# A hybrid attention block on one core: the compression in rounded floats, its second layer inside the attention loop, other places for value chunks and rotary tables, and low parts moved from GpSimd to VectorE

## The chip, the cores and the metric

The kernel runs on one core of one Trainium2 chip. The metric is the device time of one execution in microseconds (us), as the median of several runs. Names of engines: PE is TensorE, DVE is VectorE, ACT is ScalarE, POOL is GpSimd, SP is SyncE (here only a DMA queue).

## The reference

Two layers (DEPTH = 2) over 512 tokens of width 1024. Each has a mixer of two attentions and a convolutional feed-forward part:

```python
def compress_blocks(k, pe, w1, b1, w2):
    blocks = k[:, idx] + pe[None, None, :, None, :]      # 31 blocks of 32 tokens, stride 16
    flat = jnp.transpose(blocks, (0, 1, 3, 2, 4)).reshape(B, n_cmp, Hkv, CMP_BLOCK * hd)
    return jax.nn.gelu(flat @ w1 + b1, approximate=True) @ w2

def nsa_attention(...):          # 8 query heads, 2 key heads: compressed, selected and window branch
    kc = compress_blocks(k_cmp, ck_pe, ck_w1, ck_b1, ck_w2)
    vc = compress_blocks(v_cmp, cv_pe, cv_w1, cv_b1, cv_w2)
    ...
    o = g[..., 0:1] * o_cmp + g[..., 1:2] * o_slc + g[..., 2:3] * o_win

def stick_breaking_attention(q, k, v):
    ...
    log_1m = jnp.where(strict, -jax.nn.softplus(z), 0.0)
    later = lax.cumsum(log_1m, axis=3, reverse=True) - log_1m
    w = jnp.where(strict, jnp.exp(jax.nn.log_sigmoid(z) + later), 0.0)

def hybrid_mixer(h, positions, ...):
    q_nsa, kv_nsa, g_nsa, qkv_sb, g_merge = jnp.split(h @ w_in, cuts, axis=-1)
    ...                          # rotary embedding of q and of two of three keys and k_cmp
    y = g_a * (o_nsa @ w_proj_nsa) + g_b * (o_sb @ w_proj_sb)
    return y @ w_out
```

All of it is in float32.

## The kernel before

**Products.** Most matrix products run in rounded floats (`fp32r`). Each operand is split in a high part, rounded, and a low part, the rest, and a product is three matmuls: high x high, low x high, high x low. The first and second layer of the compression are an exception: they run in plain floats (line 703 and the ones behind it), for which the trace has two records per matmul.

**Weights.** `Weights` goes through one list of weight tiles in the order of use. A tile of 128 x 1024 floats comes by DMA on SP's queue into one of three buffers (`wraw`). ACT rounds it (`whi`, line 95), and DVE or POOL makes the low part (`wlo`, line 96) as the tile's item says; two buffers each for whi and wlo, or a place that the item names (`dest`: "held" slots such as `sa`, `vs0`, in which a tile stays for longer). `ensure` splits tiles ahead of their use, at high priority. The order in which each engine's instructions stand is written by a scheduler which simulates a time line and follows these priorities; an engine then runs its queue in that order.

**Stages of a layer.** (1) The head: six tiles of 128 output columns (two keys, two queries, the keys and the values to be compressed), first for 256 tokens (`head_first`), then for the others (`head_second`). In layer 0 the rotary tables are computed beside it by the generator `rope_tables`, whose steps are spread over the head's matmuls; they are written to DRAM (`rot`) and read back into `cs_t`, from which layer 1 reads them too. (2) Each of the six banks is emptied: `rope` copies it (rf, line 599), turns halves around by DMA (rs), multiplies by `cs_t` (lines 603 and 606); the last bank, with the values to be compressed, is emptied by `kd` (line 660) alone. (3) The values `vN`, from three chunks of weights; the four accumulators take the banks that come free first. (4) Two more query tiles, and the compression: 16 matmuls each for keys and values (line 703) from `cstk` and the weights `cw`, gelu into `hid`, and the second layer into `kc` and `vc`. (5) The NSA loop: 32 pieces of attention, for which POOL scales P and DVE and ACT do the rest, with projections of the next stage as fill; the scores of the compressed branch are made in its steps 0 to 3 (`cmp_scores`), their transposes in step 4. (6) Stick-breaking attention (`run_heads`): Z = scores, softplus into `sbt` (line 1027) with the diagonal masked by POOL (line 995), split in `sph` (line 1032) and `spl` (line 1033), sums on PE, exp into `sbw`, masked by POOL, split in `wh` (line 1050) and `wl` (line 1051), product with the values. Its fill is `sb_pair` (sbz, line 745; qlo and sbst, line 753) and the gates (line 766). (7) Projections and output product, (8) the feed-forward part.

Of a layer's 36 tiles of `w_m` POOL makes the low parts of 28, numbers 8 to 35; DVE makes the others. Slots have one tag each and pass from tile to tile: `vn` holds vN up to the stick-breaking stage.

## Time and profile before

| what | before |
|---|---|
| median of 3 runs | 1673.69 us (1669.89 to 1676.96) |
| profiled execution | 1679.35 us |
| span in it, first to last instruction | 1677.7 us |
| mean granted clock of PE, share of full | 0.988 |
| PE busy | 1621.3 us (97%) |
| DVE busy | 1117.1 us (67%) |
| ACT busy | 814.4 us (49%) |
| POOL busy | 280.6 us (17%) |

PE is busy nearly all the time. A busy PE is not always a fast one: a matmul counts as busy at either clock, so the granted clock has to be read beside it.

### The profile page before, as it was taken

Reading aid. Unit: us, or ns where it says so; the run is one execution under the profiler, and the core shown is the slowest. Engines: PE = TensorE matmul, PEld = TensorE weight load, DVE = VectorE, ACT = ScalarE, POOL = GpSimd, SP = SyncE. Lnnn points to the kernel's source line nnn. Section 1 sums busy time; section 2 is a strip of 40 time slices with the busy share of each in tenths; the row PEclk is TensorE's granted clock in tenths of the full one; section 3 lists DMA queues with packets and bytes.
Section 4 is the critical chain, followed back from the end, with each engine's and each line's share of the span. In section 5 each row is a group of like instructions: output and inputs, shape, how many; then the busy total and the mean of one; then the engine's idle time right before and its main releaser. Section 6 shows DMA issues by size and latency. Waiting matters only on the chain. (4 is left out here: it accounts for less than half of the span.)

```text
span 1677.7 us, 23285 instructions
## 1 busy us (share of the span) xinstructions
PE 1621.3 (97%) x9034; PEld 1402.1 (84%) x9034; DVE 1117.1 (67%) x1613; ACT 814.4 (49%) x1326; POOL 280.6 (17%) x277
## 2 busy tenths in 40 slices
PE   8999999999999999999998999999999999999997
PEld 8888887778998888888897788878789988888897
DVE  7776666767588777723757667577575697776235
ACT  4555565545554444423544555574546454444233
POOL 0135454330000000000001354454200000000000
PEclk9999999999999999999998999999999999999999
DMA  5621112113422332233655111121144133333344
GB/s 190 175 86 63 40 39 63 51 62 127 130 72 76 101 101 90 96 93 116 195 162 145 63 51 52 38 63 51 51 152 138 38 101 93 97 100 95 94 126 141
DMA packets 53358, 159.96 MB, mean 95 GB/s; under 512 B 6528, under 2 KB 12160, under 8 KB 52992
## 3 DMA queue, kind: packets, MB, share of 16 engines
q1 hardware_dynamic: 50512, 149.91, 28.8%
q10 hardware_dynamic: 1584, 4.38, 0.8%
q0 software_dynamic: 1152, 4.19, 0.7%
q8 instruction: 71, 1.16, 0.3%
q14 instruction: 39, 0.32, 0.1%
HBM read 144.82 MB, written 4.72 MB: 89 GB/s over the span
## 5 line engine op out<-in xcount | busy, mean ns | idle before, releaser
L95 ACT CAST whi<-wraw 128x1024 fp32r<-128x1024 f32 (+3 forms) x241 | 246.3, 1022 | 338.0 <-PE bk L368 256.7
L96 DVE TENSOR_TENSOR wlo<-wraw,whi 128x1024 fp32r<-128x1024 f32 (+2 forms) x185 | 217.7, 1177 | 178.7 <-ACT whi L95 176.7
L368 PE MATMUL bk<-h_hi,wlo 128*128 128x512 f32 (+1 forms) x768 | 288.4, 376 | 5.8 <-DVE wlo L96 5.8
L368 PE MATMUL bk<-h_hi,whi 128*128 128x512 f32 (+1 forms) x768 | 289.0, 377 | 4.5 <-ACT rf L599 2.4
L368 PE MATMUL bk<-h_lo,whi 128*128 128x512 f32 (+1 forms) x768 | 288.7, 376 | 2.6 <-DVE h_lo L457 2.6
L368 PE MATMUL f<-h_hi,whi 128*128 128x512 f32 x448 | 183.1, 409 | 9.3 <-DVE sbz L745 6.7
L368 PE MATMUL f<-h_lo,whi 128*128 128x512 f32 x448 | 178.5, 398 | 0.0
L368 PE MATMUL f<-h_hi,wlo 128*128 128x512 f32 x448 | 178.2, 398 | 0.0
L96 POOL TENSOR_TENSOR wlo<-wraw,whi 128x1024 fp32r<-128x1024 f32 x56 | 139.2, 2485 | 211.8 <-ACT whi L95 194.2
L368 PEld LDWEIGHTS bk<-h_hi,wlo 128*128 128x128 f32 x768 | 146.8, 191 | 32.3 <-DVE wlo L96 7.1
L368 PEld LDWEIGHTS bk<-h_hi,whi 128*128 128x128 f32 x768 | 147.2, 192 | 30.2 <-ACT rf L599 2.6
L368 PEld LDWEIGHTS bk<-h_lo,whi 128*128 128x128 f32 x768 | 146.8, 191 | 28.2 <-DVE h_lo L457 3.2
L368 PE MATMUL bk<-ah,wlo 128*128 128x256 f32 (+1 forms) x484 | 161.8, 334 | 2.5 <-DVE wlo L96 2.5
L368 PE MATMUL bk<-ah,whi 128*128 128x256 f32 (+1 forms) x484 | 160.4, 331 | 0.0
L368 PE MATMUL bk<-al,whi 128*128 128x256 f32 (+1 forms) x484 | 160.2, 331 | 0.0
L368 PEld LDWEIGHTS f<-h_hi,whi 128*128 128x128 f32 x448 | 85.4, 191 | 29.4 <-DVE sbz L745 8.1
L368 PEld LDWEIGHTS bk<-ah,wlo 128*128 128x128 f32 x484 | 91.8, 190 | 12.6 <-DVE wlo L96 3.4
L1189 DVE TENSOR_TENSOR cu<-bk,r 128x512 f32<-128x512 f32 x88 | 60.2, 687 | 61.1 <-PE bk L368 60.9
L368 PEld LDWEIGHTS f<-h_hi,wlo 128*128 128x128 f32 x448 | 85.5, 191 | 17.8
L368 PEld LDWEIGHTS bk<-ah,whi 128*128 128x128 f32 x484 | 91.9, 190 | 8.7
L368 PEld LDWEIGHTS bk<-al,whi 128*128 128x128 f32 x484 | 91.9, 190 | 8.6
L368 PEld LDWEIGHTS f<-h_lo,whi 128*128 128x128 f32 x448 | 85.5, 191 | 15.1
(233 smaller groups left out, 3252.0 us busy)
## 6 DMA issues: line engine op xcount, KB each, us to landing
wraw<-in_w_u SPq DMA_DIRECT2D x88, 512.0 KB, 3.5
wraw<-in_w_m SPq DMA_DIRECT2D x72, 512.0 KB, 3.4
wraw<-in_w_d SPq DMA_DIRECT2D x44, 512.0 KB, 3.6
wraw<-in_w_d SPq DMA_DIRECT2D x22, 384.0 KB, 3.1
wraw<-in_w_pr SPq DMA_DIRECT2D x16, 512.0 KB, 3.6
wraw<-in_w_o SPq DMA_DIRECT2D x16, 512.0 KB, 3.6
rs<-rf SPq DMA_DIRECT2D x56, 64.0 KB, 3.0
cw<-in_cw ACTq DMA_DIRECT2D x2, 1024.0 KB, 6.1
```

The costliest lines, as they stand in the source:

```text
L95: self.nc.scalar.copy(hi[:, c], raw[:, c])
L96: eng.tensor_sub(lo[:, c], raw[:, c], hi.bitcast(F)[:, c])
L368: return nc.tensor.matmul(o, a, b, start=first, stop=last, skip_group_check=True)
L1189: nc.vector.tensor_mul(u, b, r2)
```

## The change

Five things. The compression's weights become two ordinary items of the weight list, 1024 columns each, split and laid out so that the high and low part of 64 output rows stand side by side (`fold`); the moving operand is split too, so one matmul of 128 x 132 makes all four partial products, and the halves are added afterwards. The second layer (`cb`, `kc`, `vc`) moves into `finish_compression`, called in step 2 of the NSA loop, and `cmp_scores` begins in step 2, with two of its parts per step. The three value chunks get places of their own (`q1`, `on`, `sa`) and are asked for during the second half of the head. The rotary tables stay in SBUF (`rtab`, in the slot `vn`) in layer 0, and layer 1 loads them by POOL's queue; the table's computation starts eight steps later, and its first cast is placed after the last `h_lo` of the head. The six banks are taken in another order, and 15 low parts per layer move from POOL to DVE.

```diff
+            if fold:
+                t = dest(i).rearrange("p (s a c) -> p s a c", s=fold, a=2)
+                raw = raw.rearrange("p (s c) -> p s c", s=fold)
+                self.nc.scalar.copy(t[:, :, 0], raw)
+                eng.tensor_sub(t[:, :, 1], raw, t.bitcast(F)[:, :, 0])
+                self.parts[i] = t.rearrange("p s a c -> p s (a c)")
...
-        for c, n in ((0, 840), (840, 840), (1680, 560)):
-            it(w_vn[l, :, c:c + n], n)
+        for c, n, k in ((0, 840, "q1"), (840, 840, "on"), (1680, 560, "sa")):
+            it(w_vn[l, :, c:c + n], n, dest=hold(k))
         it(w_m[l, 6])
         it(w_m[l, 7])
+        for v in range(2):
+            it(cw1[l, :, v * 1024:(v + 1) * 1024], dest=hold(("vs0", "vs1")[v]), fold=16)
         for i in list(range(8, 12)) + list(range(16, 24)) + list(range(32, 36)):
-            it(w_m[l, i], eng=nc.gpsimd)
+            it(w_m[l, i], eng=nc.vector if i in (8, 9, 10) else nc.gpsimd)
         for i in list(range(12, 16)) + list(range(24, 32)):
-            it(w_m[l, i], eng=nc.gpsimd)
+            it(w_m[l, i])
...
-    def rope_tables(rt):
+    def rope_tables(rt, res, wait):
...
-        yield
-        nc.vector.tensor_copy(ang, pi_)
+        for _ in range(wait):
+            yield
+        after(nc.vector.tensor_copy(ang, pi_), last_lo[0])
...
-    def head_second(banks, kept, free=0):
+    def head_second(banks, kept, free=0, n_pre=2):
...
-            if free <= i < free + 2:
+            if free <= i < free + n_pre:
                 W.ensure(W.n_got + i - free)
...
+        rtab = slot("vn", "rtab")[:, :2 * T].rearrange("p (i t) -> p i t", i=2)
+        if l > 0:
+            nc.gpsimd.dma_start(rtab, rot)
...
         banks = [bank() for _ in range(HEAD)]
+        banks = banks[1:] + banks[:1]
...
-            cw = ip.tile([128, SLOT], F, name=nm("cw"))
-            nc.scalar.dma_start(cw, cw1[l])
...
-            nc.scalar.dma_start(cs_t, rot)
             for i in range(2):
-                nc.vector.tensor_mul(cs_t[:, i], cs_t[:, i], r2)
+                nc.vector.tensor_mul(cs_t[:, i], rtab[:, i], r2)
...
-            for i in head_second(banks, kept):
+            for i in head_second(banks, kept, n_pre=HEAD):
...
-                W.ensure(W.n_got + 1)
+                W.ensure(W.n_got + 3)
...
+            for v in range(2):
+                src = cstk[:, v].rearrange("p (m s) -> p s m", s=8)
+                nc.scalar.copy(cst[:, v, 0, :, :66], src)
+                nc.vector.tensor_sub(cst[:, v, 1, :, :66], src, cst.bitcast(F)[:, v, 0, :, :66])
...
             cps = [bank(), bank()]
             for v in range(2):
+                wt = W.get()
+                W.ensure(W.n_got)
                 for s in range(16):
-                    nc.tensor.matmul(cps[v][:64, :65], cw[:, v * 1024 + s * 64:v * 1024 + s * 64 + 64],
-                                     cstk[:, v, s:s + 513:8], start=(s == 0), stop=(s == 15))
+                    o = s // 8
+                    mm(cps[v][:, :132], wt[:, s], cst[:, v, :, s % 8, o:o + 66], s == 0, s == 15)
...
+                nc.scalar.copy(part, cps[v][64:128, :132])
+                nc.vector.tensor_add(part, cps[v][:64, :132], part)
+                nc.vector.tensor_add(sums, part[:, :66], part[:, 66:])
...
+                if n == 2:
+                    finish_compression()
                 for g_ in range(2):
                     d = n - 15 * g_
-                    if d == 0:
+                    if d == 2:
                         cg = cmp_scores(g_)
-                    if 0 <= d < 4:
+                    if 2 <= d < 4:
+                        next(cg)
                         next(cg, None)
```

What this makes of DVE's queue is shown at three places. In all rows the number behind a name is its buffer, and lines below 700 lie some 12 to 20 lines later in the changed kernel (DVE's low part, line 96, is line 106 there or line 93 for the folded weights).

DVE at the start of layer 0 before, with `h_lo` (the low part of the normed input, line 457) around the cast of the positions `rt_pi`:

```order
L432 TENSOR_TENSOR sq_177<-sq_177,sq_175 128x512
L310 CAST rt_ang<-rt_pi 128x512
L457 SCALAR_TENSOR_TENSOR h_lo<-x_71,vec_65,h_hi 128x256 x3
L311 TENSOR_SCALAR rt_ang<-rt_ang,rt_inv 128x512
L457 SCALAR_TENSOR_TENSOR h_lo<-x_71,vec_65,h_hi 128x256
L432 TENSOR_TENSOR sq_180<-sq_180,sq_177 128x512
L316 TENSOR_SCALAR rt_n<-rt_ang 128x512
```

The same place in the changed kernel, `h_lo` at line 471 and the cast at line 323:

```order
L471 SCALAR_TENSOR_TENSOR h_lo<-x_71,vec_65,h_hi 128x256 x4
L446 TENSOR_TENSOR sq_180<-sq_180,sq_177 128x512
L446 TENSOR_TENSOR sq_183<-sq_183,sq_180 128x512
L106 TENSOR_TENSOR wlo_133<-wraw_77,whi_132 128x1024
L449 TENSOR_TENSOR r_90<-sq_183 128x256
L471 SCALAR_TENSOR_TENSOR h_lo<-x_71,vec_65,h_hi 128x256 x4
L446 TENSOR_TENSOR sq_312<-sq_312,sq_298 128x512
L471 SCALAR_TENSOR_TENSOR h_lo<-x_71,vec_65,h_hi 128x256 x4
L323 CAST rt_ang<-rt_pi 128x512
```

The cast of `rt_pi` and the two rows on `rt_ang` and `rt_n` are no longer among the first half's `h_lo`; the cast stands behind the last of them.

DVE behind the head of layer 0 before, around `kd` (line 660), with the queues that each row waits for:

```order
L409 TENSOR_TENSOR rq_389<-rq_389 128x256 [waits Activation_49]
L410 SCALAR_TENSOR_TENSOR r_90<-rq_389,r_90 128x256 [waits DVE_49]
L580 COPY rT_469<-rtp_470 128x4 [waits PE_49]
L660 TENSOR_TENSOR kd_479<-bk_120,r_90 128x256x2 [waits DVE_49,DMAHW4_49,PE_49,Activation_49]
L573 TENSOR_TENSOR cs_t_465<-cs_t_465,r_90 128x512 [waits DMAHW7_49]
L573 TENSOR_TENSOR cs_t_465<-cs_t_465,r_90 128x512
L603 TENSOR_TENSOR rt_512<-rf_510,cs_t_465 128x512 [waits DVE_49,Activation_49]
L606 TENSOR_TENSOR rs_511<-rs_511,cs_t_465 128x512 [waits DMAHW3_49,DMAHW2_49,DMAHW4_49,DMAHW1_49,DVE_49]
```

The same place in the changed kernel, `kd` at line 677 and `cs_t` at line 587:

```order
L333 SCALAR_TENSOR_TENSOR rt_ang<-rt_n,rt_ang 128x512 [waits DVE_49] x3
L594 COPY rT_465<-rtp_466 128x4 [waits PE_49]
L351 TENSOR_SCALAR rt_ang<-rt_ang 128x512 [waits DVE_49]
L93 TENSOR_TENSOR wh_63_722<-wraw_589,wh_63_722 128x16x64 [waits DMAHW4_49,Activation_49]
L587 TENSOR_TENSOR cs_t_462<-rtab_107,r_90 128x512 [waits Activation_49]
L587 TENSOR_TENSOR cs_t_462<-rtab_107,r_90 128x512
L677 TENSOR_TENSOR kd_477<-bk_115,r_90 128x256x2 [waits PE_49]
```

Ahead of `kd` there now stand the last step of the tables (`rt_ang`, line 351), a low part of the compression's weights (line 93) and both rows of `cs_t`, of which the first waits for ACT and no longer for a DMA; the bank that `kd` empties is number 115 instead of 120.

DVE in the stick-breaking stage of layer 0 before, in the second of the first four heads, where one `sbz` (line 745) feeds the next fill and `wh` (line 1050) the product with the values:

```order
L1032 CAST sph_2833<-sbt_2824 128x1280
L1033 TENSOR_TENSOR spl_2834<-sbt_2824,sph_2833 128x1280
L1050 CAST wh_2799<-sbw_2793 128x1280
L753 TENSOR_TENSOR qlo_3086<-sbz_3118,sbst_3085 64x512 x2
L1051 TENSOR_TENSOR wl_2800<-sbw_2793,wh_2799 128x1280
L1027 SCALAR_TENSOR_TENSOR sbt_2888<-Z_2879,sbt_2888 128x1280
L1032 CAST sph_2897<-sbt_2888 128x1280
L1033 TENSOR_TENSOR spl_2898<-sbt_2888,sph_2897 128x1280
L1050 CAST wh_2863<-sbw_2857 128x1280
L745 SCALAR_TENSOR_TENSOR sbz_3157<-f_3126,r_90 128x512
L1062 TENSOR_TENSOR o_s_2744<-pv_2803,pvl_2812 64x512
```

The same place in the changed kernel, `sbz` at line 781, `wh` at line 1089, and DVE's low part at line 106:

```order
L1071 CAST sph_2853<-sbt_2844 128x1280
L1072 TENSOR_TENSOR spl_2854<-sbt_2844,sph_2853 128x1280
L106 TENSOR_TENSOR wlo_3133<-wraw_2751,whi_3132 128x1024
L1089 CAST wh_2819<-sbw_2813 128x1280
L789 TENSOR_TENSOR qlo_3106<-sbz_3138,sbst_3105 64x512 x2
L1090 TENSOR_TENSOR wl_2820<-sbw_2813,wh_2819 128x1280
L1066 SCALAR_TENSOR_TENSOR sbt_2908<-Z_2899,sbt_2908 128x1280
L1071 CAST sph_2917<-sbt_2908 128x1280
L781 SCALAR_TENSOR_TENSOR sbz_3177<-f_3146,r_90 128x512
L1072 TENSOR_TENSOR spl_2918<-sbt_2908,sph_2917 128x1280
```

A low part stands between `spl` and `wh` now, and the next `sbz` behind the next `sph` instead of behind `wh`. In POOL's queue of this stage only the masks are left.

## Rows read from the trace of the kernel before

**Rows 1.** Part 1 of the page: busy time, share of the span and instructions of each engine.

```profile
PE 1621.3 (97%) x9034; PEld 1402.1 (84%) x9034; DVE 1117.1 (67%) x1613; ACT 814.4 (49%) x1326; POOL 280.6 (17%) x277
```

**Rows 2.** Table by stretch of the span: start and end in us, length, then busy us (and instructions) of PE, PE's weight loads, DVE, ACT and POOL, the granted clock of PE, the share of the DMA engines, GB/s. The stretches are one at the start, the stick-breaking stage of layer 0, and the feed-forward part of layer 0.

```profile
16.00:18.00 2.00, 1.47 (x7) 1.47 (x8) 2.00 (x5) 2.00 (x6) 0.00 (x0) 0.50 0.29 55
250.00:388.00 138.00, 129.03 (x659) 107.72 (x658) 92.68 (x87) 76.36 (x78) 52.50 (x75) 0.99 0.17 54
472.00:840.00 368.00, 364.32 (x1916) 314.64 (x1915) 237.45 (x316) 162.93 (x225) 0.95 (x1) 1.00 0.34 104
```

**Rows 3.** What PE waited for, over the whole span: us in total, times, longest us.

```profile
PE bk L368 <- DVE wlo L96: 8.3, 5, 5.2
PE Z L368 <- DVE sph L1032: 7.1, 6, 1.8
PE f L368 <- DVE sbz L745: 6.7, 6, 2.3
PE bk L368 <- DVE kd L660: 3.3, 2, 2.1
```

**Rows 4.** Timeline of DVE at the start of layer 0. In this and the other timelines the columns are start and duration in us, engine, line, operation, output and inputs, shape, count, and in brackets the idle time before and what ended it.

```profile
12.00 0.43 DVE L310 CAST rt_ang<-rt_pi 128x512 f32<-128x512 int32 x1 [2.52 <-DMA rt_pi<-in_pos]
```

**Rows 5.** Timeline of PE in the same stretch.

```profile
12.88 0.39 PE L368 MATMUL bk<-h_lo,whi 128*128 128x256 f32 x1 [2.62 <-DVE h_lo L457]
...
14.08 0.41 PE L368 MATMUL bk<-h_hi,whi 128*128 128x256 f32 x1
...
20.75 0.28 PE L368 MATMUL bk<-h_hi,whi 128*128 128x256 f32 x1
...
22.43 0.28 PE L368 MATMUL bk<-h_hi,wlo 128*128 128x256 f32 x1
```

**Rows 6.** Timeline of DVE in layer 0, behind the head.

```profile
51.04 1.05 DVE L660 TENSOR_TENSOR kd<-bk,r 128x512 f32<-128x512 f32 x1 [2.02 <-PE bk L368]
54.59 1.29 DVE L573 TENSOR_TENSOR cs_t<-cs_t,r 128x512 f32<-128x512 f32 x2 [2.51 <-DMA cs_t<-rot]
```

**Rows 7.** Timeline of PE in layer 0, behind the head.

```profile
52.14 0.40 PE L368 MATMUL bk<-whi,h_hi 128*128 128x280 f32 x1 [1.20 <-DVE kd L660]
...
64.85 0.60 PE L368 MATMUL bk<-h_hi,whi 128*128 128x512 f32 x1 [2.42 <-ACT rf L599]
...
68.47 0.32 PE L368 MATMUL bk<-whi,h_hi 128*128 128x280 f32 x1
```

**Rows 8.** Timeline of DVE in layer 1, behind the head.

```profile
878.06 1.29 DVE L573 TENSOR_TENSOR cs_t<-cs_t,r 128x512 f32<-128x512 f32 x2 [8.12 <-DMA cs_t<-rot]
...
897.76 2.62 DVE L603 TENSOR_TENSOR rt<-rf,cs_t 128x512 f32<-128x512 f32 x1 [3.51 <-DMA rs<-rf]
```

**Rows 9.** Timeline of PE in layer 1, behind the head.

```profile
880.98 0.60 PE L368 MATMUL bk<-whi,h_hi 128*128 128x280 f32 x1 [2.08 <-DVE kd L660]
...
884.18 0.35 PE L368 MATMUL bk<-wlo,h_hi 128*128 128x280 f32 x1
...
902.17 0.80 PE L368 MATMUL bk<-h_hi,wlo 128*128 128x512 f32 x1 [5.21 <-DVE wlo L96]
...
908.27 0.39 PE L368 MATMUL bk<-h_lo,whi 128*128 128x512 f32 x1
```

**Rows 10.** Timeline of PE: the first and last rows of the compression's first layer in layer 0 (the matmul at 93.31 is the next piece of work), and two matmuls of 128 columns in the stick-breaking stage.

```profile
85.51 0.79 PE L703 MATMUL bk<-cstk,cw 128*64 128x65 f32 x5
...
93.31 0.50 PE L368 MATMUL f<-h_hi,whi 128*128 128x512 f32 x1
...
271.16 0.22 PE L368 MATMUL Z<-sph,nones 128*128 128x128 f32 x1
271.22 0.27 PE L368 MATMUL Z<-sph,negl 128*128 128x128 f32 x1
```

**Rows 11.** Timeline of DVE in the stick-breaking stage of layer 0.

```profile
281.96 3.03 DVE L1050 CAST wh<-sbw 128x1280 fp32r<-128x1280 f32 x1 [0.44 <-POOL sbw L995]
...
290.43 0.89 DVE L1032 CAST sph<-sbt 128x1280 fp32r<-128x1280 f32 x1 [1.20 <-POOL sbt L995]
```

**Rows 12.** Timeline of POOL (GpSimd) in the same stretch.

```profile
281.89 2.42 POOL L96 TENSOR_TENSOR wlo<-wraw,whi 128x1024 fp32r<-128x1024 f32 x1
289.37 1.03 POOL L995 TENSOR_SCALAR_AFFINE_SELECT sbt<-sbt 128x128 f32<-128x128 f32 x4 [5.06 <-DVE sbt L1027]
290.35 2.96 POOL L995 TENSOR_SCALAR_AFFINE_SELECT sbw<-sbw 128x128 f32<-128x128 f32 x4
```

**Rows 13.** Timeline of PE in the stick-breaking stage of layer 0.

```profile
297.00 0.63 PE L368 MATMUL f<-h_hi,whi 128*128 128x512 f32 x1 [2.35 <-DVE sbz L745]
...
300.41 0.50 PE L368 MATMUL f<-h_hi,wlo 128*128 128x512 f32 x1
```

**Rows 14.** Groups of instructions by line, tile and form, on DVE and POOL: output and inputs, shape, count, busy us, mean ns of one, idle before.

```profile
L96 DVE TENSOR_TENSOR wlo<-wraw,whi 128x1024 fp32r<-128x1024 f32 x155 | 189.7, 1224 | 133.4 <-ACT whi L95 131.4
...
L1032 DVE CAST sph<-sbt 128x1280 fp32r<-128x1280 f32 x16 | 26.5, 1658 | 5.5 <-POOL sbt L995 5.5
...
L1050 DVE CAST wh<-sbw 128x1280 fp32r<-128x1280 f32 x16 | 22.5, 1405 | 19.4 <-POOL sbw L995 16.1 <-PE pv L368 3.3
...
L96 POOL TENSOR_TENSOR wlo<-wraw,whi 128x1024 fp32r<-128x1024 f32 x56 | 139.2, 2485 | 211.8 <-ACT whi L95 194.2 <-PE Z L368 11.9 <-ACT pch L843 5.3
```

**Rows 15.** Part 5 of the page: the costliest group of ACT (count, busy us, mean ns of one).

```profile
L95 ACT CAST whi<-wraw 128x1024 fp32r<-128x1024 f32 (+3 forms) x241 | 246.3, 1022 | 338.0 <-PE bk L368 256.7
```

51 lines of the change are left out of this document (31 added, 20 removed).

## The prediction

> **What bounds the kernel now.** I read the page's busy times first: the reader is to see that TensorE (PE) is busy for 1621.3 of 1677.7 us, so that only 56 us of the span can be won from waits, plus what PE's own work takes too long [rows 1]. Next the table by stage: the feed-forward part of a layer has nothing to give (364.32 of 368 us), while the stick-breaking stage, 250 to 388 us, leaves PE 9.0 of 138 us idle with VectorE (DVE) busy for two thirds of it [rows 2]. Then the waits of PE by releaser: low parts of weights 8.3 us, sph 7.1, sbz 6.7, kd 3.3 [rows 3]. All of these are DVE's results, so the bound is a chain PE, DVE, PE at some twelve places. Last the timelines around each place, to see what held DVE. There the waits have a second price: after most of them the matmuls run at half their rate for some microseconds, with a granted clock of 0.50, the lower of its two levels (1.2 instead of 2.4 GHz), as between 16 and 18 us [rows 2, 5, 7, 9, 13].
>
> The sum is made against the profiled execution, 1679.35 us (span 1677.7 and 1.65 outside it). It lies 5.66 us above the median of the runs, 1673.69, and I take the same distance off at the end.
>
> **The start of layer 0.** DVE stands 2.52 us in front of the cast of the positions, whose DMA lands at 12.00 [rows 4]; h_lo is queued behind it and PE waits 2.62 us for that. From 14.08 to 20.75 PE then issues 26 matmuls of 256 columns in 6.67 us; right afterwards 14 take 1.68, or 0.12 each, at which 26 would take 3.1 [rows 5]. So the stall costs 2.62 + 3.5 = 6.1 us. In the new order the cast stands behind the last h_lo, by which time the DMA has landed. What is late next is the low part of the second weight tile (0.4 us, following the new order row by row with the trace's durations) and a stretch in which the clock must still rise: I take 4.7 of the 6.1, with 2 and 6.1 as ends.
>
> **kd in layer 0.** This is the change's own new wait. The six banks are shifted by one, so the value chunks begin on the bank that kd empties. kd starts at 51.04 today, as soon as the head's last matmul is done, and PE resumes at 52.14 after 1.20 us [rows 6, 7]. In the new order the end of the table computation, a low part of the compression's weights and both cs_t stand ahead of kd, and cs_t waits for ScalarE's sine and cosine. With the head ending near 46 us I find kd done at about 48.75, so a wait of 2.8 instead of 1.2 to 1.4, and about 0.7 us of slow matmuls behind it: -2.2 us, ends 0 and -4 (a wait of 2.4 us cost 1.35 us of slow clock, next paragraph).
>
> **rf and cs_t in layer 0.** Today cs_t waits 2.51 us for tables that go out to DRAM and come back [rows 6], the fourth rf copy on ScalarE is late by that, and PE waits 2.42 us at 64.85. It then needs 3.62 us up to 68.47 for 2 matmuls of 512 and 14 of 280 columns; at the usual 0.227 and 0.13 us that is 2.3 [rows 7]. With the tables in SBUF both go: 2.4 + 1.4 = 3.8 us, ends 0 and 3.8.
>
> **The head of layer 1.** cs_t waits 8.12 us for its DMA, which stands behind the 1 MB of compression weights on ScalarE's queue, and kd is queued behind cs_t [rows 8]. PE waits 2.08 us for kd, then runs slow until 884.18: 13 matmuls in 3.2 us, 1.7 at the usual pitch, so 1.5 more. At 902.17 it waits 5.21 us for a low part that stands behind an rt held by a DMA and then stretched to 2.62 us, and runs slow until 908.27: 14 matmuls in 6.1 us against 3.2 [rows 8, 9]. The sum is 2.1 + 1.5 + 5.2 + 2.9 = 11.7 us. In the new order the table comes in by GpSimd's queue some 30 us earlier, and the value chunks' low parts are made during the head. Followed row by row, none of these waits is left there; the tightest place has 6 us to spare. I take 11.7, ends 5 and 12.5.
>
> **The compression's matmuls.** Today 32 products per layer of 65 columns in full float take 7.8 us [rows 10]. They become 32 of 132 columns in rounded floats, whose two halves of output rows carry the high and low part of the weights. The trace has no such shape. 128 columns cost 0.06 us each from one row to the next [rows 10], 256 columns with new weights each time 0.12 [rows 5]. I take 0.11, nearer to the latter because the weights change each time: 3.5 us, gain 4.3 per layer, 8.6 in all. Ends: 1.9 us per layer at 0.06, and 7.8 (no gain) if the stretch falls to the lower clock at 0.213 or more.
>
> **The new small work.** Adding the halves (a ScalarE copy, two small DVE additions per part), the copies into aux, the split of cst, and the second layer in the attention loop. PE has the same three small products. They stand between attention tiles whose fill is ready, so nothing is queued behind them for long; their chain to the first use, the fourth step after, is 2 steps shorter than before. Cost -1 us for both layers, ends 0 and -6 (a wait of 1.5 us in each of four places).
>
> **The stick-breaking stage.** 24 of the 56 low parts that GpSimd makes leave this stage's queue for DVE, 12 per layer. Today a DVE cast that meets one of them is stretched: wh takes 3.03 us from 281.96, while the low part runs from 281.89; sph alone takes 0.89 at 290.43 [rows 11, 12]. The groups say how often: 16 sph at a mean of 1658 ns and 16 wh at 1405, against 860 undisturbed, are 16 x 0.80 + 16 x 0.55 = 21.6 us of DVE's time over both layers. Against this DVE gets 24 x 1.22 = 29.3 us of new work [rows 14]. So DVE is loaded a little more, by 4 us of 138 per layer, but a stretch of 2.1 us on the path becomes a low part of 1.2 us which mostly stands off it: the order shows it behind spl and ahead of wh, both with slack. PE's waits for sph and sbz, 7.1 + 6.7 us [rows 3], and the slow stretch from 297.00 to 300.41 (8 matmuls, 3.4 us against 1.8), once per layer, make 17 us in all [rows 13]. I take 11, since some waits for sph and sbz stay (DVE waits for GpSimd's masks as before) and the new low parts each wait for a ScalarE cast; ends -6 and 17.
>
> Here a row and a rule meet. The Trainium skill, "SBUF — State Buffer", section "SBUF: two separate sides", says that VectorE and GpSimd share one pair of ports, that it is locked for a whole instruction, and that a DVE operation with two SBUF inputs takes it as well, though only against a GpSimd operation that reads SBUF. The stretched casts agree with it (3.03 against 0.89 us). By the same rule the moved low parts, which have two inputs, can now block the masks on GpSimd: four masks take 1.03 us at 289.37 and 2.96 at 290.35 with DVE casts beside them [rows 12]. If 12 of the 24 parts each held masks on the path for their 1.22 us, 15 us would go and 1637 would become 1652; without that the sum stands.
>
> **The sum.** 4.7 - 2.2 + 3.8 + 11.7 + 8.6 - 1 + 11 = 36.6 us. 1679.35 - 36.6 = 1642.7; less 5.66 this is 1637.
>
> **Rivals.**
> - Half of it. The stick-breaking stage gives nothing back: what DVE no longer loses in stretched casts it pays for in 24 low parts, and the masks on GpSimd come later. For it: the balance of DVE is +8 us over both layers. Against it: PE's worst waits there coincide with stretches, not with a full DVE. The gain is then 25.6, and with 5 us of small waits in the attention loop 20: 1654.
> - The tables help less. If the early table or the value chunks' places come free too late in layer 1, the 11.7 us there stay: 1637 + 11.7 = 1649. For it: the tables' load waits for the slot's last reader. Against it: that reader is the matmul work of layer 0's end, some 30 us before cs_t.
> - Slower. DVE runs its queue in order, and a low part can't start before ScalarE's cast, which can't start before PE has freed one of two buffers. On GpSimd that wait cost nobody anything. On DVE each such part may hold sbt, sph or sbz back by the cast and itself, 1.02 + 1.22 = 2.24 us [rows 14, 15]. If all 24 stand on the path, this is 54 us against the other 25.6: 28 us slower, 1702. From 12 of the 24 on nothing is won. Against it: in the new order these parts stand where their cast has been done for some time, since the weights are asked for two tiles ahead.
> - No change to speak of: the stage loses some 10 to 15 us by that mechanism and the loop some more, 1673.69 - 25.6 + 20 = 1668.
>
> **How the numbers follow.** About 0.5% (8.4 us) is what a measurement here can tell from no change. The likeliest case, 1637, has 0.65, with its own range 1624 to 1648 from the terms' ends; half of it 0.15; the tables' case 0.08, no change 0.07, slower 0.05. Faster by over 0.5% (below 1665.3): 0.65 + 0.15 + 0.08 = 0.88; same 0.07; slower 0.05. The range takes in the first three: 1621 to 1661.
>
> **What would show it.** In the changed profile: no wait for h_lo near 12 us, and the head ending near 46; a wait for kd of about 3 us after it; no PE wait over 1 us between 840 and 900 and the f tile starting near 898; 32 compression matmuls in 3 to 4 us; sph and wh casts at a mean near 0.9 us with GpSimd running masks alone; no waits of 2 us at the places of 297 and 356. I am wrong if the stick-breaking stage is not shorter by 3 us or more per layer, if compression matmuls take 0.2 us, or if new waits for cmp scores, kc or vc stand in the attention loop.

## The result, and the profile after

The changed kernel takes 1655.62 us (median of four runs, 1653.63 to 1659.2) against 1674.29 us for the kernel before in the same comparison: a ratio of 0.989, with an interval of 0.9868 to 0.9912. It is faster by 1.1%. The forecast was 1637 with a range of 1621 to 1661: right in sign and inside the range, but only half of the forecast gain came. The profiled execution took 1653.88 us, 1.7 us below the median of its runs.

The page's busy times and PE's waits of the changed kernel (us in total, times, longest us):

```profile
PE 1609.0 (97%) x8970; PEld 1393.2 (84%) x8970; DVE 1118.2 (68%) x1659; ACT 825.3 (50%) x1338; POOL 211.1 (13%) x252
```

```profile
PE f L382 <- DVE gate L802: 9.2, 4, 4.0
PE bk L382 <- DVE cst L713: 3.4, 2, 1.9
PE bk L382 <- DVE wlo L106: 2.4, 3, 1.4
PE bk L382 <- ACT wh L92: 2.4, 1, 2.4
...
PE f L382 <- DVE sbz L781: 1.6, 2, 0.8
...
PE Z L382 <- DVE sph L1071: 0.5, 2, 0.3
```

The four waits of [rows 3] are gone or small: low parts 8.3 to 2.4, sph 7.1 to 0.5, sbz 6.7 to 1.6; in place of kd's 3.3 stand 2.4, once, which the view puts down to ACT. Beside them stand two that the forecast doesn't have: the evacuation of a gate tile, 9.2 us, and `cst`, the split operand of the compression, 3.4 us. So the question is not why little was won but where it went again. The table splits both profiled executions at PE's first matmul of each stage (the stick-breaking stage ends at its last product with the values); its rows add up to the end of PE's last matmul, and the 10.3 us behind that are the same in both (us).

| stretch | layer 0 before | after | layer 1 before | after |
|---|---|---|---|---|
| up to the value chunks | 52.14 | 48.47 | 36.09 | 36.13 |
| value chunks, query tiles, up to the compression | 33.36 | 31.35 | 41.20 | 30.53 |
| compression, first layer | 7.80 | 5.93 | 7.80 | 5.33 |
| attention loop, up to the first Z | 165.79 | 172.59 | 165.76 | 173.44 |
| stick-breaking stage | 125.66 | 116.13 | 126.20 | 116.12 |
| the rest of the layer | 453.59 | 453.83 | 451.93 | 452.00 |

The stick-breaking stage gives 9.5 and 10.1 us, the stretch up to the compression of layer 1 gives 10.7, and the attention loop takes back 6.8 and 7.7. The loop is read in three views of the changed kernel. First the timeline of PE in layer 0:

```profile
115.89 0.28 PE L382 MATMUL S<-cbias,identb 128*128 128x256 bf16 x1
120.19 0.80 PE L382 MATMUL f<-h_hi,whi 128*128 128x512 f32 x1 [4.01 <-DVE gate L802]
120.78 0.63 PE L382 MATMUL f<-h_lo,whi 128*128 128x512 f32 x1
...
125.36 0.40 PE L382 MATMUL f<-h_hi,whi 128*128 128x512 f32 x1
```

PE stands 4.01 us for the evacuation of the first gate tile, and the twelve matmuls from there on take 5.17 us up to 125.36, where twelve at the usual 0.227 take 2.7. DVE meanwhile:

```profile
100.33 3.50 DVE L789 TENSOR_TENSOR qlo<-sbz,sbst 64x512 fp32r<-64x512 f32 x2
...
108.84 2.22 DVE L789 TENSOR_TENSOR sbst<-sbz,sbst 64x512 fp32r<-64x512 f32 x1 [0.69 <-ACT sbst L786]
...
116.18 0.69 DVE L863 TENSOR_REDUCE cm<-cp 128x16 f32<-128x512 f32 x1 [0.63 <-ACT cp L226]
...
117.19 2.34 DVE L867 TENSOR_TENSOR cm<-cm,gates 128x16 f32<-128x16 f32 x1
119.45 0.68 DVE L802 TENSOR_TENSOR gate<-f,r 128x512 f32<-128x512 f32 x1
```

And POOL beside it:

```profile
100.39 2.89 POOL L106 TENSOR_TENSOR wlo<-wraw,whi 128x1024 fp32r<-128x1024 f32 x1
...
108.12 2.39 POOL L106 TENSOR_TENSOR wlo<-wraw,whi 128x1024 fp32r<-128x1024 f32 x1 [2.34 <-ACT whi L105]
...
117.16 2.34 POOL L106 TENSOR_TENSOR wlo<-wraw,whi 128x1024 fp32r<-128x1024 f32 x1 [0.40 <-ACT whi L105]
```

The gate's matmuls end near 115, but its evacuation stands in DVE's queue behind the softmax rows of the compressed branch (`cp`, `cm`), which now run from step 2 of the loop on. One of these works on 16 columns and takes 2.34 us, exactly as long as the low part on POOL beside it; it ends at 119.53, the low part at 119.50. Layer 1 has the same wait, 4.01 us at 935.34.

The other new wait, again in the timeline of PE, and the table by stretch behind it (start, end, length, busy us and instructions of PE, its weight loads, DVE, ACT, POOL, then granted clock, DMA share, GB/s):

```profile
79.82 6.13 PE L382 MATMUL bk<-cst,wh 128*128 128x132 f32 x32 [1.88 <-DVE cst L713]
85.75 0.73 PE L382 MATMUL f<-h_hi,whi 128*128 128x512 f32 x1
```

```profile
80.00:87.00 7.00, 7.00 (x35) 6.81 (x35) 5.73 (x9) 3.95 (x7) 0.34 (x1) 0.56 0.36 104
...
116.00:128.00 12.00, 7.99 (x26) 6.24 (x25) 6.04 (x10) 2.10 (x6) 4.14 (x3) 0.72 0.12 44
```

The 32 compression matmuls begin after an idle time and run at a granted clock near the lower level (0.56 over 80 to 87), hence 5.93 us from the first to the next piece of work instead of the forecast 3.5. In layer 1 the wait is 1.56 us and the stretch 5.33.

### The profile page after: what moved, and what is told of

It reads as the page before. It is cut to its first block, busy times and chain, and to the rows that moved or that the text cites. A ratio compares the mean times of both kernels' runs of the same rounds, so it can differ in the third digit from the quotient of the medians.

```text
span 1652.2 us, 23212 instructions
## 1 busy us (share of the span) xinstructions
PE 1609.0 (97%) x8970; PEld 1393.2 (84%) x8970; DVE 1118.2 (68%) x1659; ACT 825.3 (50%) x1338; POOL 211.1 (13%) x252
## 4 chain that ended last, share of the span: by engine, by line
PE 82%; DVE 8%; ACT 5%; issue 2%; DMA 2%; POOL 1%; SPq 1%; ACTq 0%; DVEq 0%; POOLq 0%
PE bk L382 56%; PE f L382 15%; PE pv L382 3%; PE Z L382 3%; PE S L382 2%; PE tp L935 2%; POOL sbt L1034 1%; DVE wlo L106 1%; DVE st L906 1%; DMA rs<-rf 1%; DMA x<-in_xT 1%; ACT whi L105 0%; ACT sbt L226 0%; ACT sbt L1058 0%; ACT sbw L226 0%
## 5 line engine op out<-in xcount | busy, mean ns | idle before, releaser
L105 ACT CAST whi<-wraw 128x1024 fp32r<-128x1024 f32 (+2 forms) x235 | 241.2, 1027 | 342.7 <-PE bk L382 254.3
L106 DVE TENSOR_TENSOR wlo<-wraw,whi 128x1024 fp32r<-128x1024 f32 (+2 forms) x209 | 248.8, 1191 | 184.1 <-ACT whi L105 181.4
L382 PE MATMUL f<-h_hi,whi 128*128 128x512 f32 x448 | 184.4, 412 | 11.7 <-DVE gate L802 9.2
L382 PE MATMUL bk<-h_hi,wh 128*128 128x256 f32 x512 | 96.0, 285 | 0.0
```

Source lines behind the costliest of these rows:

```text
L105: self.nc.scalar.copy(hi[:, c], raw[:, c])
L106: eng.tensor_sub(lo[:, c], raw[:, c], hi.bitcast(F)[:, c])
L382: last_mm[0] = nc.tensor.matmul(o, a, b, start=first, stop=last, skip_group_check=True)
```

## The experiments

Three questions stood after the result. Is the loop's loss due to the order of DVE's rows around the gate (theory C in the expectations), to the place of the second layer, or to the load on DVE and POOL? Is the lost gain of the compression only the late operand and the clock behind it (theory D)? And is the stick-breaking gain, nearly twice the forecast, that of the low parts, or of something else? All ratios are to the kernel before, measured beside the kernel on the same chip. No experiment leaves out work.

**Low parts put back, moved alone, and all moved.** The first undoes the move of the twelve low parts of the stick-breaking stage, the second makes this move alone in the kernel before, the third takes POOL's remaining low parts away too, the fourth gives three of them back.

```diff
 # in the changed kernel: items 12 to 15, 24 to 31
-            it(w_m[l, i])
+            it(w_m[l, i], eng=nc.gpsimd)
 # in the kernel before: the reverse, same items
 # no low parts on POOL, in the changed kernel: items 8 to 11, 16 to 23, 32 to 35
-            it(w_m[l, i], eng=nc.vector if i in (8, 9, 10) else nc.gpsimd)
+            it(w_m[l, i])
 # three back: the same items
+            it(w_m[l, i], eng=nc.gpsimd)
```

> The changed kernel with the 12 low parts per layer of the stick-breaking stage (w_m 12 to 15 and 24 to 31) back on GpSimd. Theory A (the stage's gain of 9.5 us per layer, 125.7 to 116.1 us from the first Z to the last product with the values, comes from these parts alone, because GpSimd's low parts stretch DVE's casts by 2.1 us): the stage goes back to 125 to 126 us in both layers, casts of 3.0 us return, and the time is 19 us above the changed kernel, some 1674 us. Rival (the stage is faster through the rest of the change, slots and banks): it stays at 116 to 118 us, and the time within 4 us of 1655.6.

Measured: 1684.13 us, ratio 1.0062 (1.0043 to 1.0081): slower than the kernel before. Its stick-breaking stages take 122.92 and 124.41 us, and the rest of the layers 460.77 and 458.26 where the changed kernel needs 453.83 and 452.00. But the stage holds 552 of PE's matmuls here and 588 in the changed kernel: 33 of the projections have moved out of it, into the rest. Stage and rest together, which hold the same work within three matmuls, are 13.7 and 14.5 us longer.

> The kernel before with only those 12 low parts per layer moved from GpSimd to DVE. Theory A: the stage takes 116 us in both layers instead of 125.7, the rest of the layer is as before, and the time is 19 us below before, about 1655, as fast as the whole change. Rival: without the other parts DVE's new work of 14 us per layer stands on the path, and the stage takes 122 us or more.

Measured: 1667.18 us, 0.996 (0.9944 to 0.9976); the stages 125.14 and 124.62 us, and the rest of the layer 4.5 and 4.7 us shorter than before. Here the stage holds 604 matmuls, 16 more than before, at 0.227 us each some 3.6 us of work taken out of the rest; stage and rest together are 5.0 and 6.3 us shorter.

> The changed kernel with all low parts on DVE, so also the 13 per layer that GpSimd makes in the NSA loop. Theory B (PE's new wait of 4.0 us for the first gate, once per layer, comes from three DVE instructions of the loop's start that are stretched by GpSimd's low parts: qlo 3.50, sbst 2.22, cm 2.34 us): the stretches are gone, the wait falls below 2 us, and the stretch from the compression to the first Z gets 3 us or more shorter per layer, time about 1649. Rival C (the chain kc, vc, cp, cm itself stands ahead of the gate on DVE, whatever GpSimd does): the wait stays at 3.5 us or more, and with 16 us more work for DVE per layer the time is 1656 to 1664.

Measured: 1672.98 us, 0.999 (0.9973 to 1.0007). The wait at the loop's first gate is gone, as theory B says. The loop takes 175.21 and 175.14 us and the stage 122.61 and 122.63, but 27 of the fill's matmuls, some 6.1 us, have moved from the stage into the loop (982 against 955). Counted alike, the loop is 3.5 and 4.4 us shorter than in the changed kernel, which is what theory B named, and the stage 12.6 longer.

> The changed kernel with the three low parts 8, 9 and 10 of a layer back on GpSimd, as before the change. If DVE's load between the value chunks and the loop is what PE waits for: 3.7 us less of it per layer, the waits for cst (1.9 and 1.6 us) and for the gate (4.0) shrink by 2 to 4 us per layer together, time 1648 to 1652. If a low part on GpSimd costs DVE as much in stretches as it takes away: no difference beyond 3 us either way.

Measured: 1663.51 us, 0.9949 (0.9932 to 0.9966), 8 us more than the changed kernel, which neither theory named, with a gate wait of up to 4.4 us and a `cst` wait of 4.7. The stretches hold the same work here.

What follows: the lengths of two stretches can be compared only where PE does the same work in them, and the first three of these runs move some of it. An item's engine is one of the things from which the scheduler works out its time line, so moving a low part can rewrite the order of everything around it, and the waits move with it. PE's waits with no low part on POOL show it:

```profile
PE pv L382 <- DVE wh L1089: 9.0, 4, 4.1
PE S L382 <- ACT P L226: 4.1, 4, 1.1
```

Here `wh` is late by up to 4.1 us where nothing was late in the changed kernel, though its stretches on DVE are gone. So POOL's low parts may well have a share in the loop's loss, but this run has an order of its own and doesn't show how large it is; and the low parts' own effect on the stick-breaking stage needs an order that is held.

**The gate ahead.** One edge in DVE's order: the sum of the compressed softmax comes behind the first gate's evacuation. Nothing else is edited.

```diff
-                    nc.vector.tensor_mul(at(dst, m), b, r2)
+                    g_op = nc.vector.tensor_mul(at(dst, m), b, r2)
+                if tag == "vs0" and m == 0:
+                    after(cm_add[0], g_op)
...
-                nc.vector.tensor_reduce(m[:, 1], p16, axis=AX.X, op=OP.add)
+                cm_add[g] = nc.vector.tensor_reduce(m[:, 1], p16, axis=AX.X, op=OP.add)
```

> The changed kernel with one added order on DVE: the first gate's evacuation in the attention loop stands ahead of the sum over exp(cp), so four rows earlier. Nothing else moves. Theory C (PE's 4.0 us wait for the gate is a place in DVE's queue: the gate's matmuls end near 115 us, and its evacuation stands behind the compression's softmax, which waits for ScalarE's exp and is stretched): the gate's evacuation starts near 115.4, PE's wait falls to 0.5 us or less, the slow stretch behind it goes, and the loop's loss falls by 6 us per layer, time about 1644. Rival (PE would only wait for the next thing that DVE owes it, since the chain is 6 us late anyway): another wait of 3 to 4 us appears within the next 15 us (for the transposes of cp or for st), and the time stays within 3 us of 1655.6.

Measured: 1643.41 us, 0.9827 (0.9812 to 0.9842), 12 us faster than the changed kernel by the medians and 10.5 by the two ratios. The timelines of DVE and of PE:

```profile
117.32 0.68 DVE L802 TENSOR_TENSOR gate<-f,r 128x512 f32<-128x512 f32 x1
118.03 0.69 DVE L865 TENSOR_REDUCE cm<-cp 128x16 f32<-128x512 f32 x1
```

```profile
117.75 0.28 PE L382 MATMUL S<-cbias,identb 128*128 128x256 bf16 x1
118.06 0.50 PE L382 MATMUL f<-h_hi,whi 128*128 128x512 f32 x1
```

The gate is emptied as soon as it is done and PE runs on without a wait. The loop takes 167.52 and 166.31 us, within 1.7 and 0.6 us of before, and the stick-breaking stages are unchanged (116.16 and 116.14). The loops of all three kernels hold 955 matmuls. So of the 14.5 us lost in the two loops 12.2 hang on this one order. POOL's low part makes the place in the queue dearer: without it the `cm` row ahead of the gate takes 0.17 us instead of 2.34, so about 2.2 of the 4.01 us of waiting are, by estimate from these rows, the stretch.

**The second layer in front of the loop**, with its scores from step 0 on, as in the kernel before.

```diff
+            finish_compression()
...
-                if n == 2:
-                    finish_compression()
...
-                    if d == 2:
+                    if d == 0:
-                    if 2 <= d < 4:
-                        next(cg)
+                    if 0 <= d < 4:
```

> The changed kernel with the compression's second layer ahead of the loop, and cmp_scores in steps 0 to 3, one part per step, as in the kernel before. If the place of the second layer causes the loop's loss (17.8 and 18.6 us of waits and slow matmuls against 11.0 and 10.9 before): no wait for the gate, loss back to 11 to 12 us per layer, time about 1642. If DVE is simply behind by what PE gained in the head and from the compression: the wait turns up elsewhere (kc, sbz) and the loop's loss stays above 15 us, 1652 to 1658.

Measured: 1652.61 us, 0.9886 (0.9872 to 0.9901), which these intervals can't tell from the changed kernel. Its waits:

```profile
PE f L382 <- DVE sbz L781: 5.8, 4, 2.1
PE bk L382 <- DVE cst L713: 3.6, 2, 1.9
PE S L382 <- DVE pt L946: 2.9, 2, 1.4
```

The gate's wait has gone and `sbz` and `pt` are late instead. The loops are shorter here, 167.27 and 169.41 us, but the stick-breaking stages longer, 119.43 and 119.48: a piece of the fill has moved from one to the other. The loops hold 934 matmuls instead of 955, and 21 of the fill's take 4.8 us, so of the 5.3 and 4.0 us by which they are shorter nothing is left that counts. In these two kernels the place of the second layer decides which row is late, not whether one is.

**The values first.** The values' operand of the compression is ready before the keys', which goes through a rotation and a DMA (`kd`, then `cstk`). This run takes the values first in the weight list, in the split and in the matmuls; the next one adds the gate's edge and a second edge, the first `sbz` ahead of the last query tile's `rs`; the third puts `sbz` ahead of both.

```diff
-            for v in range(2):
+            for v in (1, 0):
...
 # the second run, beside it the gate's edge
+                    if p == 0 and t == 0:
+                        after(rs_op[0], z_op)
 # the third run
+                        after(rs_op[-2], z_op)
+                        after(rs_op[-1], z_op)
```

> The changed kernel with the compression of the values ahead of that of the keys (order of the two weight items, of the two splits, and of the two groups of 16 matmuls), so that the late operand (cst of the keys, 1.9 and 1.6 us of waiting) is needed 16 matmuls later. Theory D (the 32 matmuls take 5.9 and 5.3 us only because the wait sends the clock to its lower level): the wait is under 0.5 us, the 32 matmuls take 3.5 to 4.2 us, and the time falls by 4 to 5 us per layer to about 1646. Rival (0.17 to 0.19 us is what a matmul of 128 x 132 with new weights costs): the matmuls still take over 5 us, and only the waits go, 1652.

Measured: 1657.8 us, 0.9909 (0.988 to 0.9938), not to be told from the changed kernel. The timeline of PE in layer 0:

```profile
78.74 1.90 PE L382 MATMUL bk<-cst,wh 128*128 128x132 f32 x16
81.50 1.98 PE L382 MATMUL bk<-cst,wh 128*128 128x132 f32 x16 [0.85 <-DVE cst L713]
...
88.89 0.80 PE L382 MATMUL f<-h_hi,whi 128*128 128x512 f32 x1 [4.16 <-DVE sbz L781]
```

Both groups of 16 run at 0.12 us each, at a granted clock of 1.00 over 78.7 to 83.5: the price of the matmul was right and the clock did the rest. But PE then waits 4.16 us for `sbz`, which DVE has not come to yet: the wait now comes nine microseconds later and is longer.

> The changed kernel with the first gate's evacuation ahead of the compression's softmax sum (as in the run that gave 1643 us), the values' compression ahead of the keys', and one more order on DVE: the first sbz evacuation ahead of the last query tile's rs. With the values first alone, the wait for cst had shrunk but PE stood 4.6 and 3.8 us for that sbz. If PE's waits here are places in DVE's queue, the third order takes the sbz wait away as the first took the gate's: the 32 compression matmuls take 3.5 to 4.7 us with at most 1.1 us of waiting ahead or between, no wait over 1 us from the value chunks to the gate, time 1635 to 1638. If DVE's amount of work bounds this stretch, the time stays at 1643 or rises, with the wait at another DVE result.

Measured: 1641.15 us, 0.9807 (0.979 to 0.9823), the lowest of this study, though its interval overlaps that of the gate's edge alone. Layer 0:

```profile
78.34 3.90 PE L382 MATMUL bk<-cst,wh 128*128 128x132 f32 x32
...
84.79 0.50 PE L382 MATMUL f<-h_hi,whi 128*128 128x512 f32 x1 [1.81 <-DVE sbz L782]
```

All 32 take 3.90 us at the upper clock, at 0.12 each, and what is left of the wait for `sbz` is 1.81 us (2.08 in layer 1). The expectation of no wait over 1 us and 1635 to 1638 was missed.

> The kernel with the gate ahead and the values' compression first, and the first sbz evacuation ahead of both last query tiles' rs, not only of the last one's (1641 us with that, where PE still waited 2.0 and 2.3 us for this sbz). If the wait is a place in the queue: it falls under 0.7 us in both layers, and the time to 1635 to 1638. If the query tiles' chain is late by that and what they feed is waited for: a wait for the scores or for qst in its place, 1640 to 1643.

Measured: 1645.41 us, 0.9824 (0.9806 to 0.9842), not better. In layer 1 the wait for `sbz` is gone and the next stands in its place:

```profile
905.97 0.76 PE L382 MATMUL f<-h_hi,whi 128*128 128x512 f32 x1 [6.08 <-DVE hb L743]
```

In the 26 us up to there DVE is busy for 21.5. Ahead of `hb` it stands 1.51 us for a DMA, and two `qst` rows take 3.44 beside a low part on POOL, where the two before them took 1.40. So another row is late in this order; whether DVE's amount of work or the order sets how late is not shown.

**The early tables** are put back to where they were, by the first experiment below; the second takes the banks in the old order.

```diff
-                side = Side((chain(HALVES[1], pre=g_pre), 0.6), (rope_tables(hp, rtab, 8), 0.6))
+                side = Side((chain(HALVES[1], pre=g_pre), 0.6), (rope_tables(hp, rtab, 1), 0.6))
-        after(nc.vector.tensor_copy(ang, pi_), last_lo[0])
+        nc.vector.tensor_copy(ang, pi_)
 # the second run
-        banks = banks[1:] + banks[:1]
```

> The changed kernel with the rotary tables' computation started at the first step again and without the order that puts the cast of the positions behind the last h_lo. The prediction's first step (the cast's wait for its DMA, in front of h_lo, costs the head 4.7 us): a wait of 2 to 3 us for h_lo near 12 us and a slow stretch behind it come back, the head's loss goes from 6.4 to 10 to 12 us, and the time is 4 to 6 us above the changed kernel, 1660 to 1662. Rival: the head is bound by the weights' arrival anyway, and the time stays within 2 us.

Measured: 1659.27 us, 0.9914 (0.9898 to 0.993). The stall of [rows 4, 5] is back, on DVE and on PE:

```profile
12.18 0.43 DVE L323 CAST rt_ang<-rt_pi 128x512 f32<-128x512 int32 x1 [2.81 <-DMA rt_pi<-in_pos]
```

```profile
13.06 0.58 PE L382 MATMUL bk<-h_lo,whi 128*128 128x256 f32 x1 [2.91 <-DVE h_lo L471]
```

The value chunks begin at 51.66 instead of 48.47, so the delay is worth 3.2 us there; the intervals of the whole kernels overlap.

> The changed kernel with the six banks of the head in their old order. The prediction's second step (the shifted order makes the value chunks wait for kd, 2.5 us in layer 0): the wait in front of the value chunks of layer 0 falls to 1.5 us or less, the time to about 1653. Rival (the first accumulator then waits for the rf copy on ScalarE, which is as late): a wait of 2 to 4 us for rf instead, no difference beyond 2 us, or slower.

Measured: 1654.39 us, 0.9893 (0.987 to 0.9915), the same as the changed kernel. The wait in front of the value chunks has the same length in both orders, 2.38 us:

```profile
48.87 0.50 PE L382 MATMUL bk<-wh,h_hi 128*128 128x280 f32 x2 [2.38 <-ACT wh L92]
```

The row names ACT's split of a folded weight tile; it ends at 48.77 here, and `kd` on DVE at 48.72, so either would make PE wait this long, and which of them does isn't shown. The bank order is not what makes it.

**The low parts with the order held.** Two attempts in the kernel before, with the low parts on DVE and some edges that were to hold the heads in their old order: each `wh` behind the next head's `sbt`, two products with the values behind the next head's sums, and in the second attempt two fill tiles behind the sums of heads 5 and 6:

```diff
-            it(w_m[l, i], eng=nc.gpsimd)
+            it(w_m[l, i])
...
+                    if wh_op:
+                        after(wh_op.pop(), op)
+                    if self.h in (1, 2):
+                        after(pv_op[self.h - 1], op)
 # added in the second attempt
+                    if self.h in (5, 6):
+                        after(fill_op[self.h + 1], op)
```

> The kernel before with the 12 low parts per layer of the stick-breaking stage on DVE, and with the order of the heads held as it was: on DVE each wh behind the next head's sbt, on PE the product with the values of the heads 0 and 1 behind the sums of the next head. The same move without the held order let the scheduler choose another order of the heads and gave 6 us. Theory A (the low parts on GpSimd were what held the stage): the stage's loss of waits and slow matmuls falls from 14.5 and 15.1 us to about 5 per layer as in the changed kernel, time about 1655. Rival (what gave 9.6 us per layer in the changed kernel is another part of it): the loss stays above 10 us per layer, time 1663 or more.

Measured: 1672.38 us, 0.9987 (0.9971 to 1.0003), with one wait where the fill had run out:

```profile
366.26 0.76 PE L368 MATMUL pv<-wh,vS 128*128 128x512 f32 x1 [6.04 <-DVE wh L1056]
```

> The kernel before with the 12 low parts per layer on DVE, the order of the heads held, and the last two fill tiles (gates) held back until behind the sums of the heads 5 and 6, so that fill is left for the end of the stage. With the order of the heads alone, PE had next to no wait until 360 us and then stood 6.3 us with no fill left. Theory A' (the low parts on GpSimd cost the stage about 9 us, but only an order which keeps fill to the end gets it): the stage's loss falls to 5 to 7 us per layer, time 1656 to 1659. Rival: the loss stays above 10 us, because something else of the change is needed.

Measured: 1674.05 us, 1.0002 (0.9989 to 1.0016). A part of an order is not the order: the scheduler fills in the rest in its own way. So in the next three the rows of PE and of DVE in the stage, all but DVE's low parts and one split of the projections, are chained to one written list, that of the kernel before or that of the changed kernel, in the kernel before with the low parts on either engine. Two pieces of the lists, where Z is the scores and sums of a head, W its product with the values, f the fill, and the number behind * the count of matmuls:

```
before:  Z1*12 W0*1 Z1*8 f3*7 W0*7 f3*2 Z3*8 Z2*20 f4*14
changed: Z1*18 W0*1 Z1*2 f3*9 W0*7 Z3*8 Z2*10 f4*15 Z2*10
```

In the changed order the sums with the high part of a softplus (the first Z2*10) and those with its low part have fill between them, so the low part may come later.

> The kernel before with the 12 low parts per layer of the stick-breaking stage on DVE, and the order of every matmul of the stage on PE and of every other instruction of it on DVE held exactly as in the kernel before. If the low parts alone gave the changed kernel's 9.6 us per layer: the stage's loss of waits and slow matmuls falls from 14.5 and 15.1 us to about 5, time 1654 to 1658. If the order gave it: the loss stays at 12 to 15 us, time 1668 to 1674.

> The kernel before with its low parts on GpSimd, but with the order of the stage on PE and DVE as in the changed kernel. If the order gave it: loss about 5 us per layer, time 1654 to 1658. If the low parts gave it: the stretched casts stand in front of the same waits as before, loss 13 to 16 us, time within 4 us of before.

> The kernel before with the low parts on DVE and the changed kernel's order of the stage. This should repeat the changed kernel's stage within the kernel before: loss about 5 us per layer, time 1653 to 1657, whichever of the two gave it. If the loss is above 8 us, something else of the change (slots, banks) has a part in it.

Measured, the length of the stick-breaking stage in layer 0 and 1 (us), with the time and ratio of the whole kernel:

| low parts on | order of before | order of the changed kernel |
|---|---|---|
| POOL | 125.66, 126.20 (the kernel before) | 121.01, 120.67; 1666.0, 0.9948 (0.993 to 0.9967) |
| DVE | 123.35, 122.29; 1669.54, 0.9962 (0.9942 to 0.9982) | 117.05, 117.07; 1659.9, 0.9915 (0.9894 to 0.9936) |

All hold the same work within one matmul. Down a column the low parts give 2.3 to 4.0 us per layer, along a row the order gives 4.7 to 6.3; together 8.6 and 9.1 of the 9.5 and 10.1 that the change gives. Each cell is one profiled execution; by the medians of the whole kernels the low parts give 2.6 and 3.1 per layer and the order 4.3 and 4.8, so the order gives more in both counts. The groups of DVE's casts (count, busy us, mean ns) in the run with the low parts on POOL and the new order:

```profile
L1113 DVE CAST wh<-sbw 128x1280 fp32r<-128x1280 f32 x16 | 22.4, 1400 | 8.9 <-POOL sbw L1056 8.9
L1094 DVE CAST sph<-sbt 128x1280 fp32r<-128x1280 f32 x16 | 22.2, 1389 | 10.5 <-POOL sbt L1056 10.4
```

The casts are still stretched, `wh` as much as before and `sph` somewhat less [rows 14], and the stage is 4.7 and 5.5 us shorter all the same. So a stretched cast costs less where the order leaves PE other work in front of what waits for it.

## Why the prediction was right and wrong

The step that failed is that of the new small work, which was to stand where nothing is queued behind it: it was put at 1 us and the loops lost 14.5. The terms against what the stage table and the runs show, in us:

| term | forecast | measured |
|---|---|---|
| start, kd and rf of layer 0 | 4.7 - 2.2 + 3.8 = 6.3 | 3.7 + 2.0 + 1.9 = 7.6 |
| head of layer 1 | 11.7 | 10.7 + 1.6 = 12.3 |
| compression's matmuls | 8.6 | 1.9 + 2.5 - 1.9 - 1.6 = 0.9 |
| new small work (the loops) | -1 | -6.8 - 7.7 = -14.5 |
| stick-breaking stage | 11 | 9.5 + 10.1 = 19.6 |
| the rest of both layers | 0 | -0.3 |
| sum, in the span | 36.6 | 25.5 |

The waits for `cst`, 1.9 and 1.6, lie in front of the compression's first matmul; the table counts them with the compression, to which they belong.

**The heads** came as read. No wait stands near 12 us, between 829 and 894.96 us PE waits for nothing until `cst`, and the delay of the tables alone is worth 3.2 us of the first term. `kd` was forecast as done at about 48.75 with a wait of 2.8 and slow matmuls behind it; DVE and PE show 48.32, 2.38 and no slow ones:

```profile
47.26 1.06 DVE L677 TENSOR_TENSOR kd<-bk,r 128x512 f32<-128x512 f32 x1
```

```profile
48.47 0.50 PE L382 MATMUL bk<-wh,h_hi 128*128 128x280 f32 x2 [2.38 <-ACT wh L92]
```

The reason given for that wait, the shift of the banks, was wrong: without the shift it is the same.

**The compression** had the right price, 0.12 us per matmul against 0.11 taken, and a step in front of it that had none. The DMAs that bring `cstk` are issued 8 us earlier than before, and PE comes to the compression 7.6 us earlier (it would have begun at 77.94, before at 85.51): so far both gain alike. The rows of that tile, before and after, in layer 0 (duration in ns as min/median/max, first and last start in us):

```profile
L643 SPq DMA_DIRECT2D cstk<-kd x4: 510/552/757, 80.9 to 83.2; - x4
```

```profile
L660 SPq DMA_DIRECT2D cstk<-kd x6: 507/590/599, 68.7 to 75.3; - x6
L712 ACT CAST cst<-cstk x2: 1177/1216/1255, 72.0 to 77.4; 128x528 fp32r<-128x528 f32 x2
L713 DVE TENSOR_TENSOR cst<-cstk,cst x2: 1106/1144/1183, 75.4 to 78.6; 128x528 fp32r<-128x528 f32 x2
```

But `cstk` went into the matmul itself before, and now passes through a cast on ACT and a difference on DVE, from the landing at 77.36 to 79.68: 2.3 us, on the path. This is "the split of cst", which the forecast listed among the small work that PE would not see. The 1.88 us of wait that remain of it, 1.56 in layer 1, and the low clock behind them (2.2 and 1.6 us over the 3.74 that the matmuls need) take back nearly all that the cheaper matmuls gain. The other end of this term was mis-sized: 32 matmuls at 0.213 take 6.8 us, not 7.8. The layer 1 head had been followed row by row, but not as far as this operand.

**The loop** holds the step named above: "They stand between attention tiles whose fill is ready, so nothing is queued behind them for long." What was queued behind them was the evacuation of a gate tile, the very thing that frees the fill's bank. Its end of the range was -6, from four waits of 1.5 us; two of 4.0 with twelve slow matmuls behind each came instead. The edge that puts the gate first gives 12.2 us of the loops back, which shows the cause: the gate's place in the queue. The stretch of the `cm` row ahead of it belongs to the price of that place. That the gate's row stands behind the softmax rows can be read in the order of DVE's queue alone; the forecast showed this queue at three places, and the loop was not among them.

**The stick-breaking stage** was forecast as the low parts' gain, 5.5 us per layer. They give 2.3 to 4.0. The casts came to 855 and 840 ns, as forecast:

```profile
L1071 DVE CAST sph<-sbt 128x1280 fp32r<-128x1280 f32 x16 | 13.7, 855 | 7.8 <-POOL sbt L1034 5.3 <-PE f L382 2.4
L1089 DVE CAST wh<-sbw 128x1280 fp32r<-128x1280 f32 x16 | 13.4, 840 | 9.0 <-POOL sbw L1034 8.5 <-PE pv L382 0.6
```

The greater part, 4.7 to 6.3 per layer, is the new order that the scheduler wrote for the changed kernel, which had no term. It isn't what the low parts' move alone brings about: told of that alone, in the second of the first four runs, the scheduler wrote another. That the two orders differ could be read ahead of the forecast (the next `sbz` behind `sph` instead of behind `wh`); the forecast took from it only where the low parts stand, not a gain. Which of the rows that changed places does it was not tried, and 0.9 us per layer between the chained list and the changed kernel stays open.

The rule of the Trainium skill that was weighed there ("SBUF — State Buffer", section "SBUF: two separate sides") held for the casts, 1658 and 1405 ns before and 855 and 840 after. The 15 us that it might have cost on the masks did not come: their mean rises from 472 and 413 ns to 496 and 462 in the groups of POOL, and PE's wait for sph, which comes behind a mask, is nearly gone.

```profile
L1034 POOL TENSOR_SCALAR_AFFINE_SELECT sbt<-sbt 128x128 f32<-128x128 f32 x64 | 29.4, 496 | 94.7 <-DVE sbt L1066 94.7
L1034 POOL TENSOR_SCALAR_AFFINE_SELECT sbw<-sbw 128x128 f32<-128x128 f32 x64 | 27.3, 462 | 97.7 <-ACT sbw L226 97.7
```

**The offset.** 5.66 us were taken off because the profile of before lay that far above its median. The profile of after lies 1.7 below its own, so by medians the gain is 18.7 where the spans show 25.5. Of the miss of 18.6 us, 11.1 are terms and the rest is this step: a single execution's distance to the median didn't carry over to the next kernel's.

**The range and the rivals.** The time lies outside 1624 to 1648, the likeliest case's own range. That it lies inside the whole range is in part luck: the stage gave 8.6 us more than its term and made up for some of the 13.5 and 7.7 that the loops and the compression gave less. "Half of it" named 1654, and the time is 1655.62, but by a mechanism that is the reverse of what happened: the stage that was to give nothing gave most. "Slower" needed low parts that hold DVE's rows back on the path; neither `sph` nor `wh` is late by it in the changed kernel. The tables' case did not occur.

## What to carry to other kernels

Where one engine is busy nearly all the time, time won in front of it only brings it earlier to the next operand, so each term needs a second question: is what follows ready that much sooner, with every step that the change puts in front of it? Small new work on an engine that runs its queue in order is priced by what stands behind it, above all by rows that free a buffer of the bound engine: one edge was worth 10 to 12 us here. And where a scheduler writes the order, an edit of costs or engines is also an edit of the order: hold the whole order fixed before putting a gain down to the edit, and count the bound engine's instructions in a stretch before comparing its length.
